# Hybrid attention and retention step: rows joined by a ratio, scores in three PSUM banks, a longer arena, loads in order of use

## The chip, the cores and the metric

The kernel runs on one core of one Trainium2 chip. The metric is the device time of one execution in microseconds (us). Three executions of the kernel before the change took 1957.88, 1951.35 and 1955.57 us; their median is 1955.57. A profiled execution of the same kernel took 1957.27 us, and all times of single instructions below are from that one.

The engines of a core are TensorE (PE, matmuls, with its weight loads shown apart as PEld), VectorE (DVE), ScalarE (ACT), GpSimd (POOL) and SyncE (SP), which in this kernel issues every DMA.

## The reference

One layer of a streaming encoder. 2048 prompt frames and 64 sample frames of width 1024 are RMS-normalised and multiplied by one combined weight of 6144 columns. The columns feed a differential attention (four heads; q and k in two halves of 64, values of 128), a retention with decay (four heads), a gate path for each, and two merge gates:

```python
h = rmsnorm(x, norm_g) @ w_in
qa, ka, va, za, qb, kb, vb, zb, ga, gb = jnp.split(h, _split_points(), axis=-1)
...
s = jnp.einsum('bqhcd,bkhcd->bhcqk', q, k) * (DK_A ** -0.5)
s = s - slopes * dist            # ALiBi; blocks of 64 frames are causal
p = jax.nn.softmax(s, axis=-1)
a = p[:, :, 0] - lam * p[:, :, 1]
o = jnp.einsum('bhqk,bkhe->bqhe', a, v)
...
oa = rmsnorm(oa, subln_g) * (1.0 - lam_init) * silu(za)
ob = rmsnorm(ob) * silu(zb)
m = ga * (oa @ w_oa) + gb * (ob @ w_ob)
return x + m @ w_out
```

The sample frames attend to a cache of 4096 past frames as well. Keys, values and retention states are outputs too. All is float32, and the kernel keeps that precision by splitting a factor into a high and a low part (`hi`, `lo`, as a reduced fp32 type) and making three matmuls of one: high by high, low by high, high by low.

What the change uses: with l0 and l1 the sums of the two unnormalised exponential rows u0 and u1, the attention row is u0/l0 - lam*u1/l1. The RMS norm that follows takes out any common factor of a row, except for its epsilon.

## The kernel before, in words

The kernel is a set of Python generators, one for each piece of work (a projection unit, an attention head, a softmax, an output tile). A planner (`loop`, L160) always resumes the runnable task of the best priority. Each task adds the cost of what it emits to running clocks for PE, ACT, DVE, POOL and the DMAs (`P`, `A`, `V`, `G`, `ld`, `st`), and waits by giving the time or the condition at which it may go on. `take(tag)` and `give(tag)` book a tile of a tag (a PSUM bank, a weight tile, an eviction buffer), `grab` and `drop` a stretch of columns of one long tile, the arena, for attention rows and x. The order in which the planner emits instructions is the order on PE, ACT and DVE; SP and POOL are ordered by the framework. In the program, each DMA of SP also waits for the DMA eight before it, so at most eight are under way.

The work runs in these stages.

1. Half 0 of the projections: the first 1024 prompt frames and the 64 sample frames times all weight columns. It opens with va, k (ka) and q (qa), then the retention's values vb, then q, k of the retention and the gates in Strassen units, each a 2x2 block product with seven products instead of eight. Their order and PSUM banks stand in the table `EIGHTH` (L51 on), and `ENDING` (L64) is the table for the last unit. `x_roots` (L386) loads the second half's frames and makes their RMS factors (L402 to L416: square with row sum on ACT, root, four small DVE steps). `x_scaled` (L421) loads the transposed second half, scales it (L451, L458) and splits it into high and low (L490, L492). Attention of the sample frames runs beside the units.
2. Half 1 of the projections: the same columns for the last 1024 frames, without Strassen, in two layouts: frames on the partitions (`natural`, L1064, in units of 256 columns, or 512 where `wide`) and columns on the partitions. A weight unit is loaded (`ws`), cast to its high part on ACT (`wh`, L924) and reduced to its low part on POOL (`wl`, L934). Interleaved with it runs the attention of the prompt, and the retention. The pool of the first half is closed by then and an attention zone opened (`attn_zone`, L2619), with its arena of `LATER` columns.
3. Output: the tiles of m = ga*(oa@w_oa) + gb*(ob@w_ob) (`m_tile`, L2233; matmuls L2252 to L2254), with gates made from the stored z and on; `w_o` weights are loaded and split before it (L2053, L2060). Then the final product with w_out, in Strassen form (`y_quad`, L2350).

For one attention head and one pair of 128-frame query blocks the steps are these. `qk_block` (L1453) computes, for each of the two halves c, scores for all keys in chunks of at most 512 columns: two matmuls into a bank "s" (L1469, L1470), then a DVE pass that adds the distance table (`dnear` for the last chunk, `dfar` else), writes the row to the arena and its extreme to `a_acc` (L1478). `softmax` (L1496) runs Exp with the row's sum on ACT (L1509), takes reciprocals of the sums on DVE (L1523 and near), scales the second row on ACT (L1529) and joins the two rows on DVE (L1532). `at_pv` (L1540) transposes the joined rows into a bank "at" (L1579), splits them (L1592, L1594) and multiplies by the values into bank "pv" (L1557 to L1559). `rms_t` (L1324) normalises the result over the values' axis: copy and two squares on ACT, the square's low part on DVE (L1335), a matmul with ones (L1341) into "tp", root by Ln and Exp, one correction (L1349, L1354), and the gain.

PSUM has eight banks: two each of "mm", "s" and "at", one "pv", one "tp".

`load_head` (L1377) loads K and V of a head, `load_q` (L1402) the q of one pair, `attn_tables` (L1370) the two distance tables. The tasks that call them run ahead of the attention as far as tiles are free (four K, four V, two q). The loads go through SP in the order in which the planner emits them.

Of the kernel before, what the change touches and what calls it, by code (L numbers as in the profile page):

```python
# [23 lines left out]
EPS = 1e-6  # L24
# [9 lines left out]
        "ws": 3, "w": 16, "r_o": 2, "r_sq": 2, "r_y": 1, "r_hi": 1, "r_lo": 1, "state": 1, "S": 12, "wz": 3, "qq": 1,  # L34
# [14 lines left out]
LATER = 9984  # L49
# [14 lines left out]
ENDING = EIGHTH[:4] + [("t4", 1, 4, "e", "at", None, "s_p4")] + EIGHTH[4:5] + EIGHTH[6:]  # L64
# [71 lines left out]
class Hybrid:  # L136
# [284 lines left out]
    def x_scaled(self):  # L421


        nc = self.nc
        for p in range(4):
            if p == 2:
                yield from self.take("V", 2)
                xT = [self.sb(self.ap, [128, 1024], "V", "xT") for _ in range(2)]
            else:
                xT = [span.ap for span in (yield from self.stage(p))]  # L430
            t0 = 1024 + 256 * p
            for k in range(2):
                tx = self.ld(xT[k].rearrange("p (c t) -> p c t", c=4),
                             self.i["x_prompt_T"][512 * k:512 * k + 512, t0:t0 + 256]
                             .rearrange("(c p) t -> p c t", p=128), 1 << 19)
            span = yield from self.grab(256)
            dp = span.ap
            yield lambda: len(self.rooted) >= 8
            for u in range(2):
                nc.vector.tensor_scalar(dp[:, 128 * u:128 * u + 128], self.ident,  # L440
                                        self.roots[:, 2 * p + u:2 * p + u + 1], None, op0=ALU.mult)
                t = self.V(128, self.pe)
            yield max(t, tx)
            yield from self.take("tp")
            rb = self.psum("tp")[:, :256]
            for u in range(2):
                usl = slice(128 * u, 128 * u + 128)
                nc.tensor.matmul(rb[:, usl], self.ones, dp[:, usl], start=True, stop=True)
                t = self.P(512)
            yield t  # L450
            nc.scalar.copy(dp, rb)  # L451
            t = self.A(256, t)
            self.give("tp", t)
            yield t
            for k in range(2):
                for c in range(4):
                    xc = xT[k][:, 256 * c:256 * c + 256]
                    nc.vector.scalar_tensor_tensor(out=xc, in0=xc, scalar=self.gT[:, 4 * k + c:4 * k + c + 1],  # L458
                                                   in1=dp, op0=ALU.mult, op1=ALU.mult)
                    t = self.V(300, t)  # L460
                    yield self.dve - PACE
            self.xscaled.append((xT, t))
            self.drop(span, t)
# [152 lines left out]
    def w_room(self, wide, nw, q):  # L616
# [3 lines left out]
        elif nw in (0, 2):  # L620
            tags, pool, shape = ("S", "S"), self.ap, [128, 2, 512]
        else:
            tags, pool, shape = ("w", "w"), self.wp, [128, 1, 512]
        u = q % 2 if shape[1:] == [2, 512] else 0
        if u == 0:
# [5 lines left out]
        return [w[:, u] for w in self.wroom], tags if u == shape[1] - 1 else ()  # L631

# [21 lines left out]
    def sum_prep(self):  # L654
# [18 lines left out]
        for k, (name, j, c) in enumerate(OPERANDS):  # L673
            yield from self.take("w", 2)
            h, l = (self.sb(self.wp, [128, 4, 128], "w", n, F32R) for n in ("wh", "wl"))
# [14 lines left out]
            self.spawn(self.sum_low(u, name, h, l, parts, done, k in POOLED, raw, left), 0, "w")  # L690
            yield self.act - PACE

    def sum_low(self, u, name, h, l, parts, done, pooled, raw, left):
# [9 lines left out]
        u[name] = (h, l, t)  # L703
# [89 lines left out]
    def strassen(self, dst, d0, scale=None, grouped=True, last=False):  # L793
# [5 lines left out]
        for name, src, c0, b, tag, after, fin in (ENDING if last else EIGHTH):  # L799
            yield lambda: name in u  # L800
            wh, wl, t = u[name]
# [26 lines left out]
            self.give("w", t, 2)  # L828
# [59 lines left out]
    def s_p5(self, q, ps, tag, t, dst, d0, scale, grouped):  # L888
        yield lambda: "u3" in q
        ev, t = yield from self.s_out(ps, q["c"], max(t, q["u3"]), scale)  # L890
        q["c22"] = t
# [15 lines left out]
    def s_p3(self, q, ps, tag, t, dst, d0, scale, grouped):  # L907
        yield lambda: "c21" in q
        ev, t = yield from self.s_out(ps, q["b"], max(t, q["u2"]), scale)
# [334 lines left out]
    def fin_vb(self):  # L1244
# [3 lines left out]
        def fin(ps, r, nu, t0, t, bank="mm"):  # L1248
            n, rt = 512, r
# [6 lines left out]
            self.give("ev", self.rows_out(self.vbN[t0:t0 + rt, :], raw, nu, 1 << 18))  # L1256
# [67 lines left out]
    def rms_t(self, ps, n, gain, t, tag):  # L1324
# [4 lines left out]
        self.give(tag, t2)  # L1329
# [4 lines left out]
        yield t1  # L1334
        nc.vector.tensor_sub(lo, sq, hi.bitcast(F32))  # L1335
# [11 lines left out]
        nc.scalar.activation(y, mb, AF.Ln, bias=self.epst)  # L1347
# [6 lines left out]
        nc.vector.scalar_tensor_tensor(out=sq, in0=mb, scalar=EPS, in1=sq, op0=ALU.add, op1=ALU.mult)  # L1354
# [15 lines left out]
    def attn_tables(self):  # L1370
        ap = self.ap
        self.dfar = ap.tile([128, FARW], F16, tag="dfar", name="dfar", bufs=1)
        self.ld(self.dfar, self.i["c_dfar"], 1 << 19)
        self.dnear = ap.tile([128, 512], F32, tag="dnear", name="dnear", bufs=1)
        self.ld(self.dnear, self.i["c_dnear"], 1 << 18)

    def load_head(self, half, h):  # L1377
# [5 lines left out]
        for u in range(nu):  # L1383
            usl = slice(1024 * u, 1024 * u + 1024)
            for c in range(2):
# [5 lines left out]
                ks[c][u] = k  # L1391
        for u in range(nu):
# [19 lines left out]
    def q_loader(self, half):  # L1412
        for h in range(4):
            yield from self.head_in(half, h)
            for p in range(4 * half, 4 * half + 4):
                yield from self.load_q(h, p)
# [21 lines left out]
    def attn_head(self, half, h):  # L1438
# [3 lines left out]
        for p in range(4 * half, 4 * half + 4):  # L1442
# [3 lines left out]
            pair = {"n": 0, "rows": [None, None], "t": 0.0}  # L1446
# [6 lines left out]
    def qk_block(self, h, p, b, ks, q, pair):  # L1453
# [6 lines left out]
        for c in range(2):  # L1460
            row = yield from self.grab(nk)
            accs = sp.tile([128, 8], F32, tag="a_acc", name="a_acc")
            for ci, (k0, n) in enumerate(ch):
                yield from self.take("s")
                ps = self.psum("s")[:, :n]
# [17 lines left out]
                self.give("s", t)  # L1483
# [12 lines left out]
    def softmax(self, st, nk, b, pair):  # L1496
# [17 lines left out]
        w = sp.tile([128, 2], F32, tag="a_w", name="a_w")  # L1514
        for c in range(2):
            lsum = ls[c][:, 0:1]
            if len(parts) > 1:
                lsum = sp.tile([128, 1], F32, tag="a_ls", name="a_ls")
                nc.vector.tensor_add(lsum, ls[c][:, 0:1], ls[c][:, 1:2])
                self.V(60, t)  # L1520
            nc.vector.reciprocal(w[:, c:c + 1], lsum)
            self.V(60, t)
        nc.vector.tensor_mul(w[:, 1:2], w[:, 1:2], self.nlam)  # L1523
        t = self.V(75, t)
        yield t
        for sl in parts:
            u0, u1 = (row[:, sl] for row in rows)
            n = sl.stop - sl.start
            nc.scalar.activation(u1, u1, AF.Identity, scale=w[:, 1:2])  # L1529
            t1 = self.A(n, t, 125)  # L1530
            yield t1
            nc.vector.scalar_tensor_tensor(out=u0, in0=u0, scalar=w[:, 0:1], in1=u1,  # L1532
                                           op0=ALU.mult, op1=ALU.add)
            t2 = self.V(n + 110, t1)
            self.drop(rows[1], t2, sl.start, sl.stop)
        pair["rows"][b] = rows[0]
# [3 lines left out]
    def at_pv(self, h, p, vs, tv, pair, last_pair):  # L1540
# [6 lines left out]
        pv = self.psum("pv")[:, :256]  # L1547
# [54 lines left out]
        t = done[0]  # L1602
        if last_pair:
            self.give("V", t, len(vs[0]) * 2)
        o, leave = yield from self.rms_t(pv, 256, self.gsub, t, "pv")
# [938 lines left out]
    def w_stream(self):  # L2544
# [15 lines left out]
        seq = [(vb, lambda half: self.natural(half, self.fin_vb(), False, True, half == 0), True)]  # L2560
# [16 lines left out]
        seqs = [f + seq for f in first]  # L2577
# [195 lines left out]
```

## Time and profile before

| what | before |
|---|---|
| median of three runs | 1955.57 us |
| profiled execution, its own time | 1957.27 us |
| its span, first to last instruction | 1955.5 us |
| mean granted TensorE clock | 0.985 |
| PE busy | 1893.9 us, 97% |
| DVE, ACT, POOL busy | 1269.6, 1024.7, 598.3 us |
| DMA, mean over the span | 160 GB/s |

The profiled execution took 1.8 us more than its span and 1.7 us more than the median. A line of the groups names the code line, the engine, the operation, the written tile and the read ones, the tile's size and the count. A line of the waits says which engine and line stood still, which engine and line released it, then the total time in us, the number of times and the longest. A row of the timeline gives the start, the duration and the instruction, and in brackets how long the engine had been idle and what ended that. The start times are us from the first instruction.

### The profile page before, as it was taken

What the parts mean: (1) busy time and instruction counts of PE and PEld (TensorE: products, weight loads), DVE (VectorE), ACT (ScalarE), POOL (GpSimd) and SP (SyncE); (2) the same over time, 40 slices, a digit from 0 to 9 for tenths busy, and PEclk for the clock granted to TensorE, in tenths of its full rate; (3) what the DMA queues carried; (4) which work ended last, traced back from release to release, by engine and by line L of the source; (5) the groups of instructions that cost most, each with busy time, mean ns of one, the idle gap of its engine ahead of it and who ended that gap; (6) DMA issues with size and microseconds to landing.
All of it is one profiled execution on the core that took longest, in us unless ns stands there. A gap on an engine that the chain in (4) does not pass through costs nothing. (4 is left out here: it accounts for less than half of the span.)

```text
span 1955.5 us, 33097 instructions
## 1 busy us (share of the span) xinstructions
PE 1893.9 (97%) x11434; PEld 1684.6 (86%) x11434; DVE 1269.6 (65%) x2981; ACT 1024.7 (52%) x2241; POOL 598.3 (31%) x569
## 2 busy tenths in 40 slices
PE   9899999999999599999999999999999989999999
PEld 7687888887878599998899989989999978999887
DVE  6666756755555387867775736347576369997664
ACT  6633455444434277667666745457566555554221
POOL 2520465555652022111211112211111246521442
PEclk9899999999999799999999999999999999999999
DMA  8753356555636756745425344552441278886542
GB/s 262 259 170 106 110 172 189 173 168 169 207 112 185 215 162 207 201 135 151 128 77 154 110 117 116 142 160 72 108 115 54 85 236 252 244 275 191 187 144 83
DMA packets 359273, 313.07 MB, mean 160 GB/s; under 512 B 67905, under 2 KB 315841, under 8 KB 359106
## 3 DMA queue, kind: packets, MB, share of 16 engines
q1 hardware_dynamic: 359106, 310.97, 53.4%
q8 instruction: 90, 1.47, 0.3%
q14 instruction: 77, 0.63, 0.1%
HBM read 205.43 MB, written 104.60 MB: 159 GB/s over the span
## 5 line engine op out<-in xcount | busy, mean ns | idle before, releaser
L934 POOL TENSOR_TENSOR wl<-ws,wh 128x512 fp32r<-128x512 f32 x125 | 166.7, 1347 | 421.4 <-ACT wh L924 327.7
L970 PE MATMUL mm<-xh,wh 128*128 128x512 f32 (+2 forms) x768 | 256.7, 334 | 0.0
L970 PE MATMUL mm<-xh,wl 128*128 128x512 f32 (+2 forms) x768 | 251.6, 328 | 0.6 <-POOL wl L934 0.6
L970 PE MATMUL mm<-xl,wh 128*128 128x512 f32 (+2 forms) x768 | 251.5, 328 | 0.0
L970 PE MATMUL mm<-wh,xh 128*128 128x256 f32 (+1 forms) x696 | 238.2, 342 | 0.9 <-DVE raw L1142 0.7
L970 PE MATMUL mm<-wh,xl 128*128 128x256 f32 (+1 forms) x696 | 232.5, 334 | 0.3 <-DVE xl L492 0.3
L970 PE MATMUL mm<-wl,xh 128*128 128x256 f32 (+1 forms) x696 | 232.5, 334 | 0.0
L1478 DVE CUSTOM_DVE_ANT_0 row<-s,dfar 128x512 f32<-128x512 f32 (+2 forms) x192 | 117.8, 630 | 65.7 <-PE s L1470 48.1
L1594 DVE TENSOR_TENSOR atl<-at,ath 128x512 fp32r<-128x512 f32 (+1 forms) x144 | 93.4, 658 | 96.9 <-ACT ath L1592 96.8
L970 PEld LDWEIGHTS mm<-xh,wl 128*128 128x128 f32 x768 | 144.9, 189 | 11.7 <-POOL wl L934 1.0
L970 PEld LDWEIGHTS mm<-xh,wh 128*128 128x128 f32 x768 | 145.0, 189 | 11.4 <-issue 0.2
L970 PEld LDWEIGHTS mm<-xl,wh 128*128 128x128 f32 x768 | 145.2, 189 | 11.1
L1509 ACT ACTIVATE row<-row,a_mx 128x896 f32<-128x896 f32 (+5 forms) x144 | 149.3, 1039 | 3.1 <-DVE a_mx L1488 3.0
L970 PEld LDWEIGHTS mm<-wh,xh 128*128 128x128 f32 x696 | 133.5, 192 | 14.5 <-DVE raw L1142 1.1
L970 PEld LDWEIGHTS mm<-wh,xl 128*128 128x128 f32 x696 | 133.3, 192 | 14.2 <-DVE xl L492 0.5
L970 PEld LDWEIGHTS mm<-wl,xh 128*128 128x128 f32 x696 | 133.6, 192 | 12.8
L1469 PE MATMUL s<-K,q 128*128 128x512 f32 (+3 forms) x320 | 121.1, 380 | 23.6 <-DMA q<-qT 11.9
L1592 ACT CAST ath<-at 128x512 fp32r<-128x512 f32 (+1 forms) x144 | 79.2, 564 | 102.5 <-PE at L1579 101.8
L1360 POOL TENSOR_TENSOR r_y<-r_y,r_sq 128x256 f32<-128x256 f32 x32 | 26.5, 827 | 336.4 <-DVE r_sq L1357 135.3
L1470 PE MATMUL s<-K,q 128*128 128x512 f32 (+3 forms) x320 | 116.1, 364 | 0.4 <-DMA q<-qT 0.4
L1532 DVE SCALAR_TENSOR_TENSOR row<-row,a_w 128x896 f32<-128x896 f32 (+6 forms) x88 | 94.5, 1079 | 27.5 <-ACT row L1529 27.1
L697 POOL TENSOR_TENSOR wl<-ws,wh 128x256 fp32r<-128x256 f32 x64 | 54.7, 855 | 127.1 <-ACT wh L688 116.1
(472 smaller groups left out, 5443.2 us busy)
## 6 DMA issues: line engine op xcount, KB each, us to landing
ws<-in_w_in_dram SPq DMA_DIRECT2D x160, 256.0 KB, 3.2
q<-qT SPq DMA_DIRECT2D x128, 128.0 KB, 3.0
K<-kT SPq DMA_DIRECT2D x48, 256.0 KB, 4.2
V<-vN SPq DMA_DIRECT2D x24, 512.0 KB, 5.3
row<-in_x_prompt_dram SPq DMA_DIRECT2D x16, 512.0 KB, 6.5
wz<-in_w_in_dram SPq DMA_DIRECT2D x32, 256.0 KB, 4.4
row<-in_cache_v_diff_dram SPq DMA_DIRECT2D x32, 256.0 KB, 3.1
row<-in_cache_k_T_dram SPq DMA_DIRECT2D x32, 256.0 KB, 3.2
```

What stands on the lines that cost most here:

```text
L697: nc.gpsimd.tensor_sub(l[:, cs], src, h[:, cs].bitcast(F32))
L934: self.nc.gpsimd.tensor_sub(l, st, h.bitcast(F32))
L970: nc.tensor.matmul(ps, p, q, start=c == 0 and i == 0, stop=c == KC - 1 and i == 2)
L1360: nc.gpsimd.tensor_mul(y, y, sq)
L1469: nc.tensor.matmul(ps, q1s, kk, start=True, stop=False)
L1470: nc.tensor.matmul(ps, q2s, kk, start=False, stop=True)
L1478: nc.vector.tensor_tensor_reduce(out=row[:, k0:k0 + n], in0=ps, in1=tab, scale=-SLOPES[h], scalar=3.0e38, op0=ALU.add, op1=ALU.min, accum_ ...
L1509: nc.scalar.activation(u, u, AF.Exp, bias=mx, scale=-1.0, accum_out=lp[:, k:k + 1])
L1532: nc.vector.scalar_tensor_tensor(out=u0, in0=u0, scalar=w[:, 0:1], in1=u1, op0=ALU.mult, op1=ALU.add)
L1592: nc.scalar.copy(ah[:, :w], at[:, :w])
L1594: nc.vector.tensor_sub(al[:, :w], at[:, :w], ah[:, :w].bitcast(F32))
```

## The change

- `softmax`: the ACT pass over the second row and its reciprocal scaling go. The rows are joined in one DVE step as row0 + w*row1 with w = -lam*l0/l1, that is, the row as it was, times l0. A value e = 128*EPS*l0*l0 for each row is kept for the norm's epsilon.
- `at_pv`: two transposes on PE turn the two columns e of a pair into one row in the unused half of the "pv" bank. `rms_t` adds this row to row 0 of the squares on DVE, copies it once more to the high part, and leaves out its constant epsilon; the bank is given back after that add, where it was given back after the first copy.
- `qk_block`: scores take a bank from "s" or "tp", whichever is free first.
- The arena of the attention zone grows from 9984 to 12032 columns. Of the 16 weight tiles, 12 stay in the common pool, and 4 (`wx`) lie in the pool of the first half, which is closed before half 1's attention.
- `ENDING`: the last Strassen unit's product b22 gets a bank of its own ("pv"), and is no longer made in the bank of c22. One more DVE add joins them.
- vb: in half 1 it is made as two units of 256 columns, not one of 512. In half 0 it stays wide.
- `x_roots` is spawned after the k unit of half 0, and holds one row tile at a time, where it held two.
- `x_scaled`: the loads of the transposed frames move into a task of their own, `x_stage`, which runs ahead of the scaling.
- First loads: the near table, K of head 0, the first two q, the far table, then V and the rest; before: both tables, K, V, K, V, then q.

```diff
-BUFS = {... "ws": 3, "w": 16, ...
+BUFS = {... "ws": 3, "w": 12, "wx": 4, ...
-LATER = 9984
+LATER = 12032
-ENDING = EIGHTH[:4] + [("t4", 1, 4, "e", "at", None, "s_p4")] + EIGHTH[4:5] + EIGHTH[6:]
+ENDING = EIGHTH[:4] + [("t4", 1, 4, "e", "at", None, "s_p4"), EIGHTH[4], ("b22", "S4", 0, "f", "pv", None, "s_p3")]
@@ x_roots
-            yield lambda: self.rooting < 2
+            yield lambda: self.rooting < 1
@@ x_scaled
+        self.xstaged = []
+        self.spawn(self.x_stage(), 1, "w")
+        for p in range(4):
+            yield lambda: len(self.xstaged) > p
+            xT, tx = self.xstaged[p]
@@ weight tiles
+    def either(self, n, *tags):
+        f = [self.res[tag].free for tag in tags]
+        if max(len(k) for k in f) < n:
+            yield lambda: max(len(k) for k in f) >= n
+        tag = tags[min((sorted(k)[n - 1], i) for i, k in enumerate(f) if len(k) >= n)[1]]
+        yield from self.take(tag, n)
+        return tag
+
+    def w_pair(self):
+        tag = yield from self.either(2, "w", "wx")
+        return tag, self.wp if tag == "w" else self.first
@@ rms_t
+        if eb is not None:
+            nc.vector.tensor_add(sq[0:1], sq[0:1], eb)
+            t2 = self.V(n, t1)
+            nc.vector.tensor_copy(hi[0:1], sq[0:1])
+            self.V(n)
+        self.give(tag, t2)
@@ attn_tables, load_head
-        self.ld(self.dfar, self.i["c_dfar"], 1 << 19)
+        if not self.far:
+            self.far = True
+            for p in range(2):
+                yield from self.load_q(0, p)
+            self.ld(self.dfar, self.i["c_dfar"], 1 << 19)
@@ qk_block
-                yield from self.take("s")
-                ps = self.psum("s")[:, :n]
+                bank = yield from self.either(1, "s", "tp")
+                ps = self.psum(bank)[:, :n]
@@ softmax
-            nc.vector.reciprocal(w[:, c:c + 1], lsum)
-        nc.vector.tensor_mul(w[:, 1:2], w[:, 1:2], self.nlam)
+        nc.vector.reciprocal(w[:, 1:2], l1)
+        nc.vector.scalar_tensor_tensor(out=w[:, 0:1], in0=l0, scalar=self.nlam, in1=w[:, 1:2],
+                                       op0=ALU.mult, op1=ALU.mult)
+        e = sp.tile([128, 1], F32, tag="a_e", name="a_e", bufs=8)
+        nc.vector.scalar_tensor_tensor(out=e, in0=l0, scalar=128.0 * EPS, in1=l0, op0=ALU.mult, op1=ALU.mult)
...
-            nc.scalar.activation(u1, u1, AF.Identity, scale=w[:, 1:2])
-            t1 = self.A(n, t, 125)
-            yield t1
-            nc.vector.scalar_tensor_tensor(out=u0, in0=u0, scalar=w[:, 0:1], in1=u1,
+            nc.vector.scalar_tensor_tensor(out=u0, in0=u1, scalar=w[:, 0:1], in1=u0,
                                            op0=ALU.mult, op1=ALU.add)
@@ at_pv
+        for b in range(2):
+            nc.tensor.transpose(eb[:, 128 * b:128 * b + 128], pair["e"][b], self.ident)
+            t = self.P(256)
@@ units
-        seq = [(vb, lambda half: self.natural(half, self.fin_vb(), False, True, half == 0), True)]
+        early = [(vb, lambda half: self.natural(half, self.fin_vb(), False, True, True), True)]
+        later = [(vb + 256 * g, lambda half, g=g: self.natural(half, self.fin_vb(g, 2))) for g in range(2)]
-        self.spawn(self.x_roots(), 2, "w")
+                if half == 0 and k == 1:
+                    self.spawn(self.x_roots(), 2, "w")
```

More of the change, by code (lines that the diff above doesn't have):

```diff
@@ L907, in s_p3 @@
     def s_p3(self, q, ps, tag, t, dst, d0, scale, grouped):
-        yield lambda: "c21" in q
-        ev, t = yield from self.s_out(ps, q["b"], max(t, q["u2"]), scale)
+        yield lambda: "c21" in q and (not q["last"] or "u5" in q)
+        ev, t = yield from self.s_out(ps, q["b"], max(t, q.get("u5", q["u2"])), scale)
         self.give("tlo", max(t, q["c21"]))
@@ L1242, in fin_va, with fin_vb @@
         return fin
-    def fin_vb(self):
+    def fin_vb(self, g=0, nh=4):
         nc = self.nc
@@ L1353, in rms_t @@
         yield t
-        nc.vector.scalar_tensor_tensor(out=sq, in0=mb, scalar=EPS, in1=sq, op0=ALU.add, op1=ALU.mult)
+        if eb is None:
+            nc.vector.scalar_tensor_tensor(out=sq, in0=mb, scalar=EPS, in1=sq, op0=ALU.add, op1=ALU.mult)
+        else:
+            nc.vector.tensor_mul(sq, mb, sq)
         t = self.V(n, t)
@@ L2576, in w_stream @@
                             unit(half, dst, 2 * g, None, True, fin)))
-        seqs = [f + seq for f in first]
+        seqs = [first[0] + early + seq, first[1] + later + seq]
         self.order = [[(c[0], len(c) > 2) for c in q if c[0] is not None] for q in seqs]
```

75 lines of the change are left out of this document (45 added, 30 removed), and 1 row of the table BUFS.

## The prediction

> **What bounds the kernel now.** First I read the totals and the slices on the page, then PE's waits, then stages by windows (columns: span, busy time and instructions of PE, its weight loads, DVE, ACT and POOL, granted clock, DMA share, GB/s).
>
> ```profile
> span 1955.5 us, 33097 instructions
> PE 1893.9 (97%) x11434; PEld 1684.6 (86%) x11434; DVE 1269.6 (65%) x2981; ACT 1024.7 (52%) x2241; POOL 598.3 (31%) x569
> PEclk9899999999999799999999999999999999999999
> ```
>
> PE is busy 97% of the span, so time goes only where matmuls are added or taken away, or where PE idles; idling costs twice, since the clock is below full in a few slices. The waits say where PE idles:
>
> ```profile
> PE s L1469 <- DMA q<-qT: 11.9, 1, 11.9
> PE s L1469 <- DVE a_acc L1478: 11.7, 2, 10.9
> PE tp L1174 <- DVE raw L1159: 7.3, 1, 7.3
> PE mm L823 <- DVE ev L836: 4.2, 1, 4.2
> PE s L2254 <- DVE w_o_retl L2060: 3.4, 1, 3.4
> PE s L2252 <- ACT w_o_reth L2053: 3.4, 1, 3.4
> PE at L1579 <- DVE row L1532: 0.7, 1, 0.7
> ```
>
> ```profile
> 85.00:100.00 15.00, 8.59 (x28) 7.01 (x29) 14.27 (x37) 8.24 (x22) 4.72 (x5) 0.66 0.73 233
> 592.00:603.00 11.00, 6.78 (x23) 5.19 (x22) 8.20 (x12) 2.88 (x7) 3.54 (x4) 0.69 0.70 209
> 643.00:671.00 28.00, 7.99 (x34) 7.54 (x35) 4.88 (x19) 3.58 (x12) 1.26 (x1) 0.51 0.79 233
> 671.00:1500.00 829.00, 825.48 (x5646) 767.52 (x5645) 547.19 (x1557) 529.78 (x1117) 152.37 (x126) 1.00 0.47 133
> 1593.00:1627.00 34.00, 23.86 (x152) 22.50 (x153) 28.55 (x45) 20.24 (x43) 26.44 (x22) 0.84 0.78 246
> 1627.00:1720.00 93.00, 92.83 (x750) 92.61 (x751) 89.60 (x166) 49.88 (x107) 48.74 (x42) 0.99 0.83 251
> ```
>
> Four stretches hold nearly all the loss; the long attention stage between them loses 3.5 us of 829. The lost time of a stretch is its idle time plus half of the work done at half clock. At 85 us: idle 6.4; a clock of 0.66 over 15 us means 10.2 us at half speed, of which I put 5.6 on work, so 2.8 more: 9.2. At 592: idle 4.2, 6.8 us at half speed, 5.3 of them work: 6.9. At 643: 28 less half of 7.99 is 24, and 3.1 of the 11.9 us wait lies before the window: 27. At 1593: idle 10.1, 10.9 us at half speed, nearly all work: 5.4; with 2.6 idle just before, 18.
>
> [...]
>
> **Roots later.** In the first half's projections PE waits for the normalised k at 91.42; before it stand root passes of the second half's rows:
>
> ```profile
> 76.99 0.59 ACT L1136 ACTIVATE sq<-mm 128x512 f32<-128x512 f32 x1
> 89.34 1.04 ACT L402 ACTIVATE row<-row 128x1024 f32<-128x1024 f32 x1
> 90.67 0.69 DVE L1159 TENSOR_TENSOR raw<-raw,sm_y 128x512 f32<-128x512 f32 x1
> 91.42 1.12 PE L1174 MATMUL tp<-ident,raw 128*128 128x128 f32 x4 [7.32 <-DVE raw L1159]
> ```
>
> The squares are made at 76.99, the product they feed only at 90.67, with root passes on ACT and their DVE steps between. The change spawns the roots after k and one at a time: eight ACT passes of 1.04 us with four small DVE steps each, and eight 512 KB loads on SP, move past this point into the wide vb projection, where PE waits for no such result. Gain 9 (0 if the sample rows' own chain is late anyway; 9.2 if all goes).
>
> **The last Strassen unit.** Its b22 product must wait for the bank of c22:
>
> ```profile
> 592.63 3.42 DVE L492 TENSOR_TENSOR xl<-row,xh 128x512 fp32r<-128x512 f32 x2
> 595.98 0.68 DVE L836 TENSOR_TENSOR ev<-mm,u 128x512 f32<-128x512 f32 x1
> 596.71 0.80 PE L823 MATMUL mm<-S4h,wh 128*128 128x512 f32 x1 [4.22 <-DVE ev L836]
> ```
>
> The eviction stands behind 3.42 us of x splitting. With a bank of its own (pv, idle then) b22 waits for nothing: gain 6.9. The one more DVE add (0.68) is hidden by half 1's matmuls. Next late is the splitting of x itself, which has 6.9 us less time; in the changed order all four splits of the last quarter follow the third va group, where two went ahead before. I take +2; ends 0 and 6.9, when the gap merely moves.
>
> **First loads of attention.** PE reaches the first score before q has landed, then stands on a cast and the scores' DVE work behind it:
>
> ```profile
> 623.12 0.35 SPq L234 DMA_DIRECT2D dfar<-in_c_dfar_dram  x1
> 657.45 0.41 SPq L239 DMA_DIRECT2D vN<-thi  x1
> 662.85 0.58 ACT L1189 CAST thi<-tp 128x512 fp32r<-128x512 f32 x1 [27.60 <-DMA vN<-thi]
> 666.38 0.58 PE L1469 MATMUL s<-K,q 128*128 128x256 f32 x1 [10.87 <-DVE a_acc L1478]
> ```
>
> ```profile
> 605.00:640.00 35.00, 34.29 (x283) 1.00 0.71 183
> 623.00:652.00 29.00, 17.13 (x143) 16.92 (x141) 3.40 (x9) 3.95 (x8) 3.80 (x3) 0.85 0.92 212
> ```
>
> By the sizes in the code, two tables (0.7 MB), two heads' K (2.0 MB) and V (2.0 MB) went ahead of q (0.5 MB); after, the near table, one head's K and the first q are 1.8 MB. At the 212 GB/s of the window that is 8.5 us; with landing I take 10 us after the loads begin, and they begin 21 us into half 1 (623.1, with the last matmul of half 0 at 602). But the program puts the first score 198 narrow matmuls into half 1 where it was 297: at 34.29/283 = 0.121 us, 24 us in. So PE still waits some 7 us. The second wait stays in kind: the store of vN, whose buffer the cast needs, is again behind the same bytes in SP's queue, and DVE's score work is behind the cast's consumer. It comes after about 20 us of other matmuls, so I estimate 8 of idling and 4 of half clock. 27 becomes 19: gain 8, ends 0 (the same bytes set the second wait) and 20 (only the first stays).
>
> **The join without a scaling pass, three banks, longer arena.**
>
> ```profile
> L1529 ACT ACTIVATE row<-row,a_w x88: 389/988/1371, 674.1 to 1530.5; 128x768 f32<-128x768 f32 x20, 128x896 f32<-128x896 f32 x20, 128x1024 f32<-128x1024 f32 x16, 128x640 f32<-128x640 f32 x8
> L1532 DVE SCALAR_TENSOR_TENSOR row<-row,a_w x88: 344/1142/2373, 675.6 to 1531.7; 128x768 f32<-128x768 f32 x20, 128x896 f32<-128x896 f32 x20, 128x1024 f32<-128x1024 f32 x16, 128x640 f32<-128x640 f32 x8
> L1335 DVE TENSOR_TENSOR r_lo<-r_sq,r_hi x32: 407/420/1530, 692.7 to 1550.9; 128x256 fp32r<-128x256 f32 x32
> L1349 ACT ACTIVATE r_sq<-r_y x32: 416/417/421, 696.4 to 1553.4; 128x256 f32<-128x256 f32 x32
> 900.63 0.49 PE L1579 MATMUL at<-ident,row 128*128 128x128 f32 x3
> 900.87 0.36 PE L1469 MATMUL s<-K,q 128*128 128x256 f32 x1
> L1579 PE MATMUL at<-ident,row x544: 270/272/330, 684.9 to 1546.7; 128*128 128x128 f32 x182
> ```
>
> ACT loses 88 passes, 87 us; PE had waited for the join only 0.7 us, so directly this is worth nothing, at most the stage's 3.5 us. DVE keeps the 88 joins, adds an add and a copy per pair (64 x 0.42 = 27 us) and swaps reciprocals for short scalar ones; it was busy 547 of 829, which hides it. The banks are worth nothing by the same 3.5 us. The epsilon row costs PE 64 transposes: three took 0.24 us from start to start, 0.08 each, or 5.1; the median duration of 0.272, if nothing overlaps, gives 17.4. I take 6, near the row of pipelined ones. The pv bank is now held for two ACT squares and the DVE add, 2 x 0.417 + 0.42 = 1.25 us longer per pair; behind it wait the next pair's value matmuls, while other tasks' matmuls fill PE. Between 0 and 32 x 1.25 = 40 I take 3, since PE waited for values once, 1 us, in the whole stage.
>
> [...]
>
> **Earlier attention, later projections.** With arena and ACT freed, more attention goes ahead and more projection matmuls stand after the last value matmul: in the changed order 120 of 320 columns, 120 of 256 and 102 of 512, against 72, 60 and 48; at 0.15 (between), 0.121 and 0.233 us that is 56 us instead of 29. Under them the output weights load and convert (the two 3.4 us waits), and the first gates load. 18 us are lost here; but DVE is busy 89.60 of 93 in the next stretch and 28.55 of 34 in this one, so part of the wait is DVE's and comes back. I take two thirds, 12; ends 0 and 18.
>
> **vb in two units, fewer weight tiles.** 384 matmuls at 0.121 replace 192 of 512 columns:
>
> ```profile
> 590.00 0.39 PE L823 MATMUL mm<-S1h,wl 128*128 128x512 f32 x1
> 592.10 0.40 PE L823 MATMUL mm<-S1h,wl 128*128 128x512 f32 x1
> ```
>
> Nine steps in 2.10 us are 0.233 each. 46.5 - 44.8 = +1.7. Half 1 prefetches one and a half units of weights instead of two; I take 0 and price it below. The separate x loads are as many as before and move from the scaling's queue place forward; 0, in SP's idle.
>
> **Sum.** -9 - 6.9 + 2 - 8 + 6 + 3 - 12 + 1.7 = -23.2. The profiled run was 1957.27 us, 1.8 over its span and 1.7 over the median of 1955.57. 1957.3 - 23.2 = 1934, 1.1% below the median. The likeliest case's own range is 1926 to 1946. A measurement here tells 0.3% (5.9 us) from no change.
>
> **Rivals.** *The waits come back:* the 8 us of the opening return (both waits come from one queue's bytes) and of the 12 at the output only 4 stay, DVE being full there: 1950. For it: 96% DVE at 1627 to 1720. Against: fewer bytes before the first q.
> *All of it goes:* 9.2 + 6.9 + 20 + 18 less 1.7 and 5.1: 1910. Against it the 24 us at which the first score now comes.
> *Transposes in series:* 64 x 0.19 more, 1946.
> *Weights late (slower):* half 1 has 24 units.
>
> ```profile
> L924 ACT CAST wh<-ws x128: 601/620/640, 6.7 to 1527.9; 128x512 fp32r<-128x512 f32 x128
> L934 POOL TENSOR_TENSOR wl<-ws,wh x125: 1262/1296/1929, 7.4 to 1528.6; 128x512 fp32r<-128x512 f32 x125
> ```
>
> A piece takes 0.62 on ACT and 1.30 on POOL after a tile is free. With 12 tiles the second half of a unit is converted only while the unit before it ends; if ACT is then in softmax the unit starts 1 to 2 us late, 24 to 48 in all: 1958 to 1982. It decides from 1 us per unit on, over most units. Against it: POOL worked 152 of 829 us there.
> *The pv bank (slower):* the whole 40 instead of 3: 1971.
> *It does not do what it says:* the banks and arena are not what binds and the order shifts elsewhere; no change.
>
> **Chances.** As summed 0.45; waits back 0.18; all gone 0.08; series 0.07; weights 0.14; pv 0.05; nothing 0.03. Faster: 0.45 + 0.08 + 0.07 + 0.08 of the second = 0.68; within 0.3%: the other 0.10, 0.03 and 0.02 of the weights = 0.15; slower 0.17. The range 1914 to 1962 leaves out half of "all gone", most of the weights and pv: 0.2.
>
> **What would show it.** Right: no L1159 wait near 90 us; no L823 wait at the half; first score about 24 us into half 1 with one wait near 7, a second on L1478 near 8; output waits of 6 us in all; L1469 and L970 without new waits. Wrong: waits of mm L970 on wl or wh (weights), of pv L1559 on the r_o or sq chain (bank), the transposes 0.27 apart, or the 592 wait returning as one for L492.

## The result, and the profile after

The changed kernel takes 1927.25 us (median of four runs, 1924.92 to 1934.06), the kernel before, measured beside it, 1956.45. The ratio is 0.986, with a 95% interval of 0.983 to 0.989. The prediction was 1934 in a range of 1914 to 1962. The profiled execution of the changed kernel took 1928.47 us, with a span of 1926.5.

The totals of the changed kernel's page, and its slices of granted clock:

```profile
span 1926.5 us, 33600 instructions
PE 1896.9 (98%) x11690; PEld 1696.0 (88%) x11690; DVE 1283.2 (67%) x3046; ACT 949.6 (49%) x2153; POOL 598.7 (31%) x569
PEclk9999999999999999999999999999999999999999
```

PE is busy 3 us longer in 29 us less time. ACT has lost 75 us of work, DVE has 14 more. The longest of PE's waits, changed kernel:

```profile
PE s L1514 <- DMA q<-qT: 5.2, 2, 4.2
PE tp L1201 <- DVE raw L1186: 3.3, 2, 2.2
PE mm L997 <- ACT raw L1166: 3.0, 2, 1.9
PE tp L1372 <- DVE r_hi L1364: 2.9, 1, 2.9
PE s L1514 <- DVE a_acc L1523: 1.8, 4, 0.7
PE at L2302 <- DVE ogl L2258: 1.7, 1, 1.7
PE mm L997 <- ACT xh L499: 1.7, 1, 1.7
```

(L1514 is the score's first matmul, L1201 the transpose of the normalised k or q, L997 the projection, L1372 the norm's matmul with ones, L2302 the output tile's second matmul. Where L1514 waits for `a_acc` it waits for a score bank: the DVE pass L1523 reads the bank and so frees it. L1469 and L1478 are the same pair in the kernel before.) The wait of the last Strassen unit (L823 before) and the two on the output weights are gone. The wait on q, 11.9 us before, is 4.2 at its longest.

Where the time went is read from four stages: half 0 of the projections, then half 1 with attention, then the output tiles, then the last product. The windows of the kernel before, with the columns as in the prediction:

```profile
0.00:601.60 601.60, 585.32 (x2694) 475.26 (x2695) 382.80 (x822) 285.87 (x708) 274.00 (x314) 0.99 0.57 175
601.60:1578.60 977.00, 949.76 (x6503) 885.35 (x6502) 604.02 (x1679) 587.58 (x1230) 173.62 (x143) 0.99 0.48 135
1578.60:1787.50 208.90, 194.72 (x1536) 192.51 (x1535) 178.80 (x344) 109.57 (x233) 88.28 (x73) 0.97 0.79 240
1787.50:1955.50 168.00, 164.13 (x707) 131.46 (x705) 103.97 (x137) 41.66 (x71) 62.38 (x39) 1.00 0.47 155
```

And of the changed kernel:

```profile
0.00:593.00 593.00, 584.50 (x2694) 474.61 (x2695) 377.43 (x820) 285.22 (x707) 272.51 (x313) 0.99 0.59 177
593.00:1570.00 977.00, 961.68 (x6758) 903.43 (x6757) 636.71 (x1758) 520.88 (x1158) 187.40 (x151) 0.99 0.50 140
1570.00:1759.20 189.20, 187.26 (x1537) 186.62 (x1536) 164.69 (x331) 101.84 (x218) 76.61 (x66) 1.00 0.81 242
1759.20:1926.50 167.30, 163.45 (x707) 131.38 (x705) 104.39 (x139) 41.68 (x71) 62.18 (x39) 1.00 0.47 155
```

Half 0 is 8.6 us shorter, the output tiles 19.7. The middle, which holds the new join, the banks, the arena and the first loads, takes 977.0 us in both: it idles 12 us less (27.2 before, 15.3 after) and pays this with 12 us more busy time, of which 8.4 are matmuls that were not there and 3.6 half clock. The gain at the output comes with less DVE work in that stage, 164.7 us instead of 178.8, and no lost clock. Where that work went, two more windows show: from the last value matmul to the first output tile, before,

```profile
1549.50:1578.60 29.10, 29.10 (x186) 27.18 (x185) 9.56 (x13) 12.86 (x25) 9.09 (x7) 1.00 0.62 185
```

and after:

```profile
1514.20:1570.00 55.80, 55.80 (x350) 51.69 (x349) 20.80 (x26) 27.52 (x53) 26.46 (x20) 1.00 0.72 214
```

The output weights' first load is issued just behind the last value matmul in both, at 1549.77 and 1514.53. I call the stretch behind it the cover: projections that PE does while DVE, ACT and POOL prepare the output.

### The profile page after: what moved, and what is told of

The parts are those of the page before. It is cut to its first block, busy times and chain, and to the rows that moved or that the text cites. A ratio compares the mean times of both kernels' runs of the same rounds, so it can differ in the third digit from the quotient of the medians.

```text
span 1926.5 us, 33600 instructions
## 1 busy us (share of the span) xinstructions
PE 1896.9 (98%) x11690; PEld 1696.0 (88%) x11690; DVE 1283.2 (67%) x3046; ACT 949.6 (49%) x2153; POOL 598.7 (31%) x569
## 5 line engine op out<-in xcount | busy, mean ns | idle before, releaser
L961 POOL TENSOR_TENSOR wl<-ws,wh 128x512 fp32r<-128x512 f32 x125 | 171.8, 1387 | 412.8 <-ACT wh L951 326.2
L997 PE MATMUL mm<-xh,wh 128*128 128x512 f32 (+2 forms) x768 | 257.3, 335 | 0.0
L997 PE MATMUL mm<-wh,xh 128*128 128x256 f32 (+1 forms) x760 | 251.4, 331 | 4.7 <-ACT raw L1166 3.0
L997 PE MATMUL mm<-xh,wl 128*128 128x512 f32 (+2 forms) x768 | 251.6, 328 | 0.0
L997 PE MATMUL mm<-xl,wh 128*128 128x512 f32 (+2 forms) x768 | 251.5, 327 | 0.0
L997 PE MATMUL mm<-wh,xl 128*128 128x256 f32 (+1 forms) x760 | 245.2, 323 | 0.3 <-DVE xl L501 0.3
L997 PE MATMUL mm<-wl,xh 128*128 128x256 f32 (+1 forms) x760 | 244.7, 322 | 0.0
L997 PEld LDWEIGHTS mm<-wh,xh 128*128 128x128 f32 x760 | 147.2, 194 | 16.5 <-ACT raw L1166 3.6
L997 PEld LDWEIGHTS mm<-wl,xh 128*128 128x128 f32 x760 | 147.3, 194 | 10.9
L997 PEld LDWEIGHTS mm<-wh,xl 128*128 128x128 f32 x760 | 146.6, 193 | 11.4 <-DVE xl L501 0.5
L997 PEld LDWEIGHTS mm<-xh,wh 128*128 128x128 f32 x768 | 145.0, 189 | 10.7
L997 PEld LDWEIGHTS mm<-xl,wh 128*128 128x128 f32 x768 | 145.2, 189 | 10.3
L997 PEld LDWEIGHTS mm<-xh,wl 128*128 128x128 f32 x768 | 144.8, 189 | 10.6
L1523 DVE CUSTOM_DVE_ANT_0 row<-s,dfar 128x512 f32<-128x512 f32 (+2 forms) x146 | 90.5, 636 | 44.9 <-PE s L1515 38.4
L1514 PE MATMUL s<-K,q 128*128 128x512 f32 (+3 forms) x242 | 91.6, 380 | 7.0 <-DMA q<-qT 5.2
L951 ACT CAST wh<-ws 128x512 fp32r<-128x512 f32 x128 | 77.2, 619 | 35.2 <-PE mm L997 15.9
```

Source lines behind the costliest of these rows:

```text
L951: self.nc.scalar.copy(h, st)
L961: self.nc.gpsimd.tensor_sub(l, st, h.bitcast(F32))
L997: nc.tensor.matmul(ps, p, q, start=c == 0 and i == 0, stop=c == KC - 1 and i == 2)
L1514: nc.tensor.matmul(ps, q1s, kk, start=True, stop=False)
L1523: nc.vector.tensor_tensor_reduce(out=row[:, k0:k0 + n], in0=ps, in1=tab, scale=-SLOPES[h], scalar=3.0e38, op0=ALU.add, op1=ALU.min, accum_ ...
```

## The experiments

Each kernel was timed four times or more beside the kernel before. Unless said otherwise, its edit is made in the changed kernel; its time, a median, compares with 1927.25, and its ratio to the kernel before with 0.983 to 0.989.

The changed kernel with the first loads in their old order deadlocks, so it has no time, and what the old order costs there is open.

**1. The roots back.**

```diff
-            yield lambda: self.rooting < 1
+            yield lambda: self.rooting < 2
...
-                if half == 0 and k == 1:
-                    self.spawn(self.x_roots(), 2, "w")
+        self.spawn(self.x_roots(), 2, "w")      # before the first unit
```

> The changed kernel with the root passes of the second half's rows back where they were (spawned before the first unit, two at a time). Theory 1 (the passes stand ahead of the k chain on ACT and DVE): the wait of tp on the normalised k near 85 us grows from 2.2 to about 7 us with half clock behind it, half 0 gets about 6 us longer, 1933. Rival (the wait belongs to the k chain itself): it stays near 2 us, and the waits at 123 and 143 us, which came with the move, go: 1924.

1932.94 us, ratio 0.989 (0.987 to 0.990). The wait on k is back at its old size, in this kernel's waits:

```profile
PE tp L1201 <- DVE raw L1186: 7.4, 1, 7.4
```

Half 0 takes 596.7 us instead of 593.0. The passes did stand in k's chain: the wait is 7.4 us with them and 2.2 without. The move is worth some 4 us in half 0, by one trace of each kernel. The medians differ by 6 us, but their intervals overlap.

**2 and 3. The roots later still**, after the q unit and after vb (`k == 2`, `k == 5`).

> The changed kernel with the root passes one unit later still, spawned after the q unit. Theory (the waits at 123 and 143 us in the changed kernel are its root passes now standing in the q chain on ACT and DVE): these waits of 1.2 and 1.9 us and the half clock after them go, the one at 85 stays: 1923 to 1925. Rival (they belong to the q chain, as the one at 85 does to k's): no change, 1927.

> The changed kernel with the root passes spawned after the vb unit, so that they fall among the Strassen units. Theory: as with roots after q, 1923 to 1925, unless the Strassen evictions on DVE and ACT are delayed, which would show as waits of mm L847 on L860. Rival: no change, 1927.

1928.33 (0.983 to 0.987) and 1934.37 (0.988 to 0.991). The rival holds: the projection's wait on raw near 143 us stays and grows to 2.5, and the one near 122 stays at 1.15, though the first root pass now starts at 183.7. They belong to q's own chain. After vb the roots come too late for the splitting of x: new waits of 2.9 us at 601 (L457) and 1.3 at 611 on x's high part. Of the two times, the first can't be told from the changed kernel's, and the second's interval overlaps with it.

**4. b22 in the bank of c22.** `ENDING` and the three lines in `s_p5` and `s_p3` as before.

> The changed kernel with the last Strassen unit's b22 back in the bank of c22. Theory 1 (the bank wait was a loss of its own): the wait of 4.2 us before S4 with its half clock comes back, about 6.9 us, 1934. Rival (the gap only moved to the splitting of x): the wait on x's cast at 612 us (1.7 us, and 3.4 us of half clock behind it) goes with it, net 3 to 4, 1930.

1945.40 us, ratio 0.996 (0.994 to 0.997), 18 us worse and not by what either theory said. Its waits:

```profile
PE s L1511 <- DVE a_acc L1520: 25.2, 2, 24.8
PE mm L847 <- DVE ev L860: 4.1, 1, 4.1
```

The bank wait is back, 4.1 us, and the wait on x's cast at 612 is gone, as the rival had it: half 0 is 3.3 us longer. But the planner also put the first score 15 matmuls earlier, and one wait of 24.8 us appeared there. Its chain, from this kernel's timeline:

```profile
637.74 0.38 SPq L239 DMA_DIRECT2D vN<-thi  x1
643.04 0.59 ACT L1242 CAST thi<-mm 128x512 fp32r<-128x512 f32 x1 [33.25 <-DMA vN<-thi]
644.15 0.69 DVE L1246 TENSOR_TENSOR tlo<-mm,thi 128x512 fp32r<-128x512 f32 x1 [33.64 <-ACT raw L1244]
645.10 0.58 PE L1511 MATMUL s<-K,q 128*128 128x256 f32 x1 [24.82 <-DVE a_acc L1520]
```

The store of vN is issued at 637.74, behind the first loads, and ACT stands 33 us before the cast that waits for it. The step on DVE behind that cast stands ahead of the passes that free the score banks. All three banks are full by then, and PE stops. In the kernel before, the wait of 10.9 us near 666 had the same chain. So in half 0 the bank of its own is worth some 3 us, and the total of this run cannot be read as its price: an edit in half 0 moved the order of half 1.

**5. Two banks.**

```diff
-                bank = yield from self.either(1, "s", "tp")
+                bank = "s"; yield from self.take(bank)
```

> The changed kernel with scores in the two banks s alone. In its order the projection matmuls left after the last value matmul are 27.6 us instead of 56.6, with arena and join as changed. Theory 1 (what covers the output weights' loading is that work): the waits on w_o and ogl come back as before, 12 to 18 us, 1940 to 1945. Rival (the order of loads in SP's queue or the freed ACT removed them): no such waits, 1927 to 1929. If banks cost waits at the scores as well, those show on L1514.

1953.22 us, ratio 0.998 (0.997 to 1.000): nearly the whole gain gone by one line. Three windows of this kernel, the middle, the output tiles and the cover:

```profile
592.10:1564.40 972.30, 959.69 (x6759) 902.73 (x6758) 634.20 (x1744) 511.70 (x1140) 179.71 (x143) 0.99 0.49 135
1564.40:1782.10 217.70, 198.37 (x1537) 193.87 (x1536) 179.97 (x347) 111.76 (x236) 92.00 (x74) 0.95 0.78 234
1537.00:1564.40 27.40, 27.40 (x173) 25.42 (x172) 7.05 (x12) 11.84 (x23) 10.55 (x8) 1.00 0.57 165
```

and four of its waits, three at the output and the one on a score bank:

```profile
PE s L2302 <- DVE ogl L2258: 7.3, 5, 4.7
PE s L2303 <- DVE w_o_retl L2109: 3.8, 1, 3.8
PE at L2301 <- ACT ogh L2255: 3.5, 1, 3.5
PE s L1514 <- DVE a_acc L1523: 0.3, 1, 0.3
```

The waits at the output come back, as theory 1 had it, and cost more than it forecast. The middle is even 4.7 us shorter than with three banks: with two, PE waited 0.3 us in all for a score bank. What the third bank changes is the order. Scores are emitted earlier, attention ends 23 us earlier (1514 against 1537), and 56 us of projections are left over instead of 27. Without them the output stage takes 28.5 us more.

**6. The old join**, `softmax`, `at_pv` and `rms_t` of the kernel before, with three banks and the arena kept.

> The changed kernel with the old softmax, the scaling pass on ACT and the constant epsilon back (no e rows, no 64 transposes, no added adds), three banks and the arena kept; 53.7 us of projections stay after the last value matmul. Theory 1 (the join itself is worth nothing to PE and costs 64 transposes, 6 us): PE's net work falls by 5 to 6 us, no new waits, 1921 to 1923. Rival (ACT's 87 us were needed): waits of at L1626 on the join and of s on DVE appear, 1935 to 1945.

1925.84 us, ratio 0.984 (0.982 to 0.987): no difference from the changed kernel that these runs can tell. PE's work in the middle falls by 7 us as theory 1 had it (64 fewer transposes), and no wait on the join appears, with ACT's 88 passes back. But the cover is 53 us, and the output stage takes 195.7 instead of 189.2 us, so the 7 us go there. The new join, with ACT's 87 us freed and the transposes paid, is thus worth nothing that these runs can tell.

**7. The new join alone**, in the kernel before.

> The kernel before with the new join alone (ratio, epsilon rows, no scaling pass). In its order only 8 us of projections lie between the last value matmul and the first output tile, against 29 in the kernel before. Theory (from the runs with two banks and the short arena: loss at the output 2 us at 56 us of cover, 12 to 14 at 41, 18 to 26 at 27 to 29): the output stage loses more than before, 25 to 40, and 64 transposes add 7: 1965 to 1985, slower than before. Rival (the freed ACT is worth something by itself): 1945 to 1955.

1973.51 us, ratio 1.009 (1.008 to 1.011): slower than before. Its waits:

```profile
PE s L2267 <- ACT ogh L2221: 19.3, 3, 14.8
```

and the cover, of which PE works 8.46 us:

```profile
1571.00:1594.20 23.20, 8.46 (x61) 7.93 (x59) 6.04 (x9) 11.46 (x25) 7.66 (x7) 0.74 0.77 243
```

PE stands 14.8 us before the first output tile, and its net work in the middle is 6 us more, about the price of the transposes. Against that, the waits on the first q and the score behind it are 3 us shorter.

**8. A short arena**, `LATER = 9984`.

> The changed kernel with the arena of 9984 columns again; 41.6 us of projections after the last value matmul. After the run with two banks the theory is: the output stage's waits depend on how many us of projections lie between the last value matmul and the first output tile (27 to 29 us: 18 to 26 lost; 56 us: 2). At 41.6 I expect 5 to 8 us lost there, 1933. Rival (a threshold near 35 us: once the output weights are in, all is hidden): 2 us lost, 1927. Another (the arena matters to the scores' own waits): waits in the attention stage.

1930.41 us, ratio 0.988 (0.986 to 0.990). The cover is 41.2 us and the output stage takes 199.5, 10 us more than in the changed kernel. That is more than the 5 to 8 expected, and the rival with a threshold near 35 us falls. The median is only 3 us higher, with overlapping intervals: half 0 and the middle of this trace are shorter by 6 us together.

**9 and 10. The first loads.** Once the far table, near table, K and V of head 0 go before the first q; once q of pair 0 goes right behind half of K.

```diff
-        if not self.far: ... load_q(0, 0), load_q(0, 1), dfar      # before the V loop
+        if not self.far: ... load_q(0, 0), load_q(0, 1)            # after the V loop; dfar first of all
```

```diff
-        self.ld(self.dnear, self.i["c_dnear"], 1 << 18)
...
+                if not self.far and c == 0:
+                    yield from self.load_q(0, 0)
...
-            for p in range(2):
-                yield from self.load_q(0, p)
+            self.ld(self.dnear, self.i["c_dnear"], 1 << 18)
+            yield from self.load_q(0, 1)
```

> The changed kernel with 1.5 MB more ahead of the first q: the far table first, then the near one, K and V of head 0, then q. The first score is 29 us of work into half 1 (24 in the changed kernel). Theory 1 (q waits for the bytes ahead of it at some 210 GB/s): 7 us later, of which 5 are covered: the wait of 4.2 becomes 6 to 7, and the waits after it stay: +2 to +4, 1931. Rival (order does not matter, the queue of eight does): no change of the wait, 1927.

> The changed kernel with less ahead of the first q: K of the first half c, q of pair 0, K of the second half, near table, q of pair 1, far table, V. 0.5 MB instead of 1.3 before q. Theory 1: q lands 3.5 us sooner, its wait of 4.2 us goes to 1 to 2 (the first score comes 1 us earlier too) and the half clock with it, the second wait near 652 stays: 1923. 76 us of projections after attention: nothing lost at the output. Rival (the wait moves to the second half's K or to the near table's DVE pass): 1927.

1932.39 (0.987 to 0.991) and 1933.40 (0.986 to 0.992). Waits of the later loads:

```profile
PE at L1626 <- DVE row L1576: 6.0, 1, 6.0
PE s L1514 <- DMA q<-qT: 5.9, 1, 5.9
```

and with q first (where the score lines stand one higher):

```profile
PE tp L1372 <- DVE r_hi L1364: 7.6, 1, 7.6
PE s L1515 <- DMA K<-kT: 2.1, 1, 2.1
```

In both, the first wait goes as the bytes ahead of q say: 5.9 us with 1.5 MB more, and two of 1.6 and 0.9 us on q with 0.8 MB less. With q first, though, K is late next, and the second wait grows from 2.9 to 7.6. With the later loads it is 6.0, at another line; there the output stage, behind a cover of 41.9 us, takes 10 us more, and the middle is no longer than the changed kernel's. Both intervals overlap with the changed kernel's, so that either order is slower is not shown; that q first brings the 4 us that theory 1 forecast is not borne out.

**11. No epsilon rows.** No transposes of e, no add, no copy. The constant epsilon is added although the rows still carry the factor l0, so this kernel leaves out epsilon's right weight. It prices the epsilon rows and does not replace them.

> The changed kernel without the epsilon rows: no transposes of e, no add and copy in the norm; the constant epsilon is applied to the unnormalised result instead, so that epsilon has a slightly wrong weight. 72 us of projections after attention. Theory (64 transposes cost 7 us of PE, 0.11 each, and nothing else): PE's net work in the middle falls by 7, the output loses nothing: 1920. Rival (they overlap with loads of weights and cost 0.08 or less): 1922 to 1924; another (the held pv bank costs as well): below 1916.

1919.76 us, ratio 0.982 (0.980 to 0.983). Its middle:

```profile
591.00:1558.60 967.60, 953.58 (x6694) 897.45 (x6693) 618.91 (x1697) 524.69 (x1161) 194.21 (x153) 0.99 0.51 142
```

64 matmul-type instructions fewer and 8.1 us less busy time than the 961.68 of the changed kernel; without the 0.9 us that I put down to half clock, 7.2 us, or 0.11 for each transpose. Nothing is left over for the held bank.

**12. One transpose for each pair**, meant to keep epsilon's right weight at half the transposes.

```diff
+        if pair["e"][0] is None:
+            pair["e"] = [sp.tile([128, 2], F32, tag="a_e", name="a_e", bufs=8)]
+        e = pair["e"][0][:, b:b + 1]
...
-        for b in range(2):
-            nc.tensor.transpose(eb[:, 128 * b:128 * b + 128], pair["e"][b], self.ident)
+        nc.tensor.transpose(eb, pair["e"][0], self.ident)          # eb: two rows
...
-            nc.vector.tensor_add(sq[0:1], sq[0:1], eb)
+            for b in range(2):
+                s2 = sq[0:2, 128 * b:128 * b + 128]
+                nc.vector.scalar_tensor_tensor(out=s2, in0=eb, scalar=self.ident[0:2, b:b + 1], in1=s2,
+                                               op0=ALU.mult, op1=ALU.add)
```

> A version that would beat both: the changed kernel with both blocks' e side by side in one tile, so that one transpose per pair (32 in all, not 64) brings them into two rows of the pv bank, added by two masked DVE steps. Theory (a transpose costs PE 0.11 us and nothing else): PE's net work in the middle falls by 3.6, the order leaves 71 us of projections after attention: 1921 to 1925. Rival (the price was the held bank, and the second DVE step holds it longer): 1927 to 1930.

1922.91 us, ratio 0.984 (0.982 to 0.986). The median is 4.3 us below the changed kernel's, about what the 32 transposes saved would make (PE's net work in the middle is 3.9 us less), but the intervals overlap: that it is faster is likely and not shown.

The cover and the output stage of all kernels timed (each from its own trace: last value matmul to first output tile, first to last output tile):

| kernel | cover, us | output stage, us | median, us |
|---|---|---|---|
| new join alone | 23.2, of which 8.5 work | 210.2 | 1973.51 |
| two banks | 27.4 | 217.7 | 1953.22 |
| before | 29.1 | 208.9 | 1956.45 |
| short arena | 41.2 | 199.5 | 1930.41 |
| loads later | 41.9 | 199.2 | 1932.39 |
| old join | 52.8 | 195.7 | 1925.84 |
| roots after q | 55.7 | 191.7 | 1928.33 |
| roots after vb | 55.8 | 188.7 | 1934.37 |
| changed | 55.8 | 189.2 | 1927.25 |
| roots back | 55.8 | 189.9 | 1932.94 |
| one transpose | 70.6 | 189.8 | 1922.91 |
| no epsilon rows | 70.9 | 192.7 | 1919.76 |
| q first | 76.6 | 191.0 | 1933.40 |
| b22 in c22's bank | 79.1 | 191.0 | 1945.40 |

From 27 to 56 us of cover the output stage shortens by 28.5 us, about one for one, if not evenly (the old join has 3 us less cover than the changed kernel and 6.5 us more output); beyond that nothing more comes. Edits of several kinds set the cover (banks, arena, join, loads, the last Strassen unit); no run changed it and nothing else, so that it is the cause is inferred from this row of kernels and from the DVE work that moved, not shown by itself.

## Why the prediction was right, point by point

The measured 1927 lies in the range and, by a little, in the likeliest case's own (1926 to 1946), and the sign was right; the terms were not all right, and their errors partly cancelled. By stage the forecast was -15.9 in half 0, +4.7 in the middle and -12 at the output; the traces show -8.6, 0.0 and -19.7. That the sums, -23.2 and -29.0, lie so near each other is in part luck.

- *Roots, -9.* Right in mechanism, too large. Half 0 lost only 3.7 us when they were put back. The prediction gave the wide vb projection no wait on such a chain; PE, 7 us earlier, then met q's chain (1.15 and 1.94 us, and a clock of 0.51 from 143.70 to 147.10 behind the second). At k itself 2.2 of the 7.3 us stay.
- *Last Strassen unit, -6.9, and +2 for x's splitting.* The wait went. The splitting was late by 1.7 and 0.3 us, and the clock behind it was 0.50 for 3.4 us (614.78 to 618.20), all of them work, so +3.7. Together some 3, against 4.9 forecast. Half 0 and this wait: -16 forecast for the two gains, 8.6 found in half 0.
- *First loads, -8.* Mis-sized, in the safe direction. The first wait is 4.2 and 0.5 us where I took 7. The second was said to stay in kind, 8 us of idling and 4 of half clock. It stayed in kind and cost 2.9 and some 1.5 (clock 0.50 from 652.33 to 655.74, PE busy 3.05 us of it). With the half clock behind the first wait (0.50 from 625.02 to 631.85, PE busy 5.62 us of it) the opening loses some 12 us where the forecast left 19, so the gain there is some 15. The long stretch behind it, which the forecast left alone, loses 7 us instead of 3.5. The changed kernel's timeline on that place:

```profile
625.75 0.44 PE L1514 MATMUL s<-K,q 128*128 128x128 f32 x1 [4.21 <-DMA q<-qT]
...
650.61 0.58 ACT L1216 CAST thi<-tp 128x512 fp32r<-128x512 f32 x1 [5.43 <-DMA vN<-thi]
651.83 0.40 DVE L1362 TENSOR_TENSOR r_sq<-r_sq,pv 1x256 f32<-1x256 f32 x1
652.27 0.28 DVE L1364 CAST r_hi<-r_sq 1x256 fp32r<-1x256 f32 x1
652.69 0.55 PE L1372 MATMUL tp<-r_hi,ones 128*128 128x256 f32 x1 [2.89 <-DVE r_hi L1364]
```

  The cast waits for the store of vN behind the loads, as forecast (5.43 us, where it was 27.60), and PE waits for DVE's work behind it. That this work is now the new epsilon add (L1362) says nothing of that add's price: with the old join PE waits 6.1 us at the same place.
- *Transposes, +6; the pv bank, +3; vb in two units, +1.7.* PE's net work in the middle rose by 8.4. The transposes are 0.11 us each: between the 0.08 of the pipelined row and the 0.27 of the duration, near the first. The rows of the transposes alone would have misled:

```profile
L1650 PE MATMUL pv<-ident,a_e x64: 270/273/275, 643.6 to 1514.4; 128*1 128x128 f32 x64
```

  The duration is 0.273, but without the 64 transposes PE's work in the middle fell by only 7.2 us (experiment 11), where 64 durations make 17.5: they overlap with their neighbours, and the rival in which the transposes run in series falls. No cost of the bank shows.
- *Output, -12.* The term that failed most: -19.7. Nearly all of the 18 us of waits and half clock went (idle 14.2 us before, 1.9 after; clock 0.97 and 1.00). The forecast kept a third because DVE was full there; but DVE's own work of that stage fell by 14 us, since it moved under the longer cover.
- *Why the cover grew.* The prediction named the arena and the freed ACT. Taken out of the changed kernel one at a time, the arena costs 14.6 us of cover (41.2 with the short one), the join 3, and the third bank, which the prediction counted as worth nothing, 28, and with them all of the gain at the output. Added alone to the kernel before, the join takes 20 us away. The losses come to more than the 27 us gained, so they do not add up, and each holds for this order of the planner only. Worth nothing for the waits of the scores was right in the long stage; that banks change the order of emission was missed. The 56 us themselves had been read from the changed order, and so the forecast came out without its cause.
- *Weights, 12 tiles, 0.* Right: no wait of L997 on wl or wh stands among the changed kernel's, and the rival that late weights make it slower falls.
- *Rivals.* "The waits come back" fell with the output. "All of it goes" came true for the output alone. The slower ones had no trace. "It does not do what it says" was half right: the banks did not bind, and the order did shift, but to the gain of the output.

Sum of the stages, with the last product: -8.6, 0.0, -19.7, -0.7 make -29.0 of span.

## What to carry to other kernels

In a kernel whose order a planner writes, look first at what a resource does to the order: here a third PSUM bank for scores, for whose lack PE stood 0.3 us in all, was worth 26 us, and a join that takes 87 us of work from ACT nothing that the runs can tell. When the next stage begins with loads and conversions, count the bound engine's work that is left to cover them; that number (29 us before, 56 after) went with the output stage better than any engine's load, up to 56 us. It is not the whole: the kernel with the longest cover, 79 us, lost 24.8 us at its first scores. And an edit that takes time out of one stage sends every chain behind it onto PE earlier: here about half of the two waits removed in half 0 came back in the next chains.

## What the runs showed of the hardware

In the changed kernel PE waited 1.94 us for ACT (L997 on L1166) until 143.25. The clock was 1.00 from 140.30 to 143.70 and 0.51 from 143.70 to 147.10 (columns: span, PE busy and count, clock, DMA share, GB/s):

```profile
140.30:143.70 3.40, 1.46 (x7) 1.00 0.67 171
143.70:147.10 3.40, 3.40 (x10) 0.51 0.41 144
```

In the kernel without epsilon rows the same wait of 1.94 us ended at 141.59, and the clock stayed at 1.00:

```profile
138.00:141.40 3.40, 1.65 (x9) 1.00 0.45 126
141.40:144.80 3.40, 3.21 (x14) 1.00 0.58 185
144.80:148.20 3.40, 3.40 (x18) 1.00 0.30 63
```

PE worked through the 3.40 us at 0.51, so that I estimate the price of that stretch as half of them, 1.7 us on top of the wait. In the other trace the same wait cost nothing more. What decides between the two is not shown; for pricing a wait, the two traces give 1.9 us with 1.7 more, or with nothing.
